# The first norm of a two-layer trunk: its squares, its sums and the loading of its rows

## Chip, core and metric

The kernel runs on one core of a Trainium2 chip. The metric is device time in microseconds (us). The engines are TensorE (PE: matmuls, with weight loads shown apart as PEld), VectorE (DVE), ScalarE (ACT), GpSimd (POOL) and SyncE (SP, which here only issues DMAs). L272 is line 272 of the kernel before.

## What is computed

A trunk of two layers over 512 tokens with 1024 features. Each layer is a mixer (layer 0: HGRN2 beside RWKV7; layer 1: attention), an MLP and a gate. What the change touches is the first step of layer 0, the RMS norm of the input and the projections behind it:

```python
def rms_norm(x, g, eps=NORM_EPS):
    xf = x.astype(jnp.float32)
    y = xf * lax.rsqrt(jnp.mean(xf * xf, axis=-1, keepdims=True) + eps)
    return (y * g.astype(jnp.float32)).astype(x.dtype)
...
    h = rms_norm(x, attn_norm[l])
    ...
    u = (h @ w_in).astype(jnp.float32)   # the input of both mixers
```

## The kernel before

The activations are kept with the features on the partitions: `x[k]`, k = 0 to 7, is a tile of 128 features by 512 tokens (256 KB), here called a row of the input. Matmuls of full precision are made of three passes: each operand is split into a high half, rounded on ACT (`act` L272, weights `whi` L228), and a low half, the remainder, made on DVE (L273, `wlo` L229); `mm3` (L235) then multiplies high by high (L236), high by low (L237) and low by high (L238). One output tile of a projection takes 8 x 3 matmuls of 512 columns. They are summed over the 8 rows in a PSUM bank (`pj` has 2 banks, `pmh` 2, `pmr` 4).

The norm isn't applied before the projections. The rows are split with only the gain as a scale. The projections run on them, and the reciprocal root of the mean square, one number for each token, is multiplied in when a projection is evacuated (`mixed` L417, `proj_h` L851). For this it is needed as a broadcast tile `rb` (128 x 512).

The sum of squares is formed in two steps. `NormAcc.add` (L301) squares a row, on ACT (L304) for odd k and on DVE (L306) for even k. The first square is the accumulator, and POOL adds the seven others to it (L310). The squares after the first come from the ring `E`, which has 4 buffers. At the end `NormAcc.rs` makes one `Stats` with one `add` (L281): four matmuls, with 128 tokens of the accumulator as weights and a column of ones as the moving operand, so that PSUM has the sums with the tokens on the partitions. Each of these four leaves two records in the trace. A dozen small DVE operations (L292 and `rsqrt`, L253) make the reciprocal root, four transposes on PE (L325) broadcast it, and ACT copies it to `rb` (L334). Other norms of the kernel use the same classes; `NormAcc` stays in use there.

Loading: one tile of weights is two pieces of 256 KB (`wnext`, L214), each issued on SP's queue and then split. There are two buffers for raw pieces (`wr`) and three for split ones. SP issues in this order: the vectors, x0, the first weight piece, x1 and x2, the second piece, x3 to x7, then the weights that follow. POOL's queue loads the constants and masks, and POOL first clears several tiles (L375, L378).

The order of the instructions on each engine is made ahead of the run by a scheduler, which takes what is ready by its own account of time, first in the program first, and gives out the buffers of the pools. At run time each engine keeps to this order and waits where something is not ready. The program's order around the change is: loads, split and square of each row, the end of the norm, masks (L399 on), the two LoRA projections (L840, `first` is the weight tile that was loaded early), then `proj_rkv(0)` (L876), `pre_h(0)` and `p1(0, 0)` of the first RWKV head (L898), and the rest of layer 0 in `step` (L899). `pre` (L456) starts with a matmul (L463) on the evacuated first LoRA projection `lwa`; in it the key norm `kk` goes through a `Stats` of its own (L474), `rsqrt` and transposes.

Of the kernel before, what the change touches and what calls it, by code (L numbers as in the profile page):

```python
# [17 lines left out]
AF = mybir.ActivationFunctionType  # L18
# [159 lines left out]
def trunk(ctx, tc, wts, xT, pT, vecs, lora, cst, lev, seg, rope, out, upto="all", dbg=None, mode=None):  # L178
# [97 lines left out]
    class Stats:  # L276
        def __init__(self, pool, tag, cols=1):
            self.n, self.cols, self.i = 1, cols, 0
            self.ps = pool.tile([P, 512], F32, name=tag)
# [48 lines left out]
    def norm_finish(st, tag):  # L328
        return norm_rows(st.rs(tag))

    def norm_rows(rt):
        ps = bcast_rows(rt, 1, pmh, "pmh")
        rb = nrm.tile([P, S], F32, name="rb")
        A.copy(rb, ps)  # L334
        return rt, rb
# [17 lines left out]

    # ------------------------------------------------------------------ layer 0: mixers
    def layer0_mixer(actp):
# [15 lines left out]
        SB = mp.tile([P, 9, P], F32, name="SB")  # L371
        PP = mp.tile([P, 4, P], F16, name="PP")
        early = [BH, KAs, *NAs, *BZ, GB, SB, PP]
        for t in early[:NE]:
# [4 lines left out]

        # norm of the input  # L380
        nc.sync.dma_start(vec, vecs)
        rest = iter(range(8))

        def load(n):
            for _ in range(n):
                k = next(rest)
                nc.sync.dma_start(x[k], xT[:, k, :])
        load(X0)
        first = wnext("in", WI["l", 0], lambda: load(X1))
        load(8 - X0 - 2 * X1)  # L390
        xs = []
        st = NormAcc(E)
        for k in range(8):
            xs.append(split(actp, x[k], "act", vcol("an0", k)))
            st.add(x[k], "act" if k % 2 else "dve")
        rt, rb = norm_finish(st, "n")

        # masks
        m32 = mp.tile([P, 14 * P // 4], I32, name="m32")  # L399
# [56 lines left out]
        def pre(hp, r, k, v):  # L456
            lw = E("lw", 2, [P, 3, P])
            ld = nc.gpsimd.dma_start(lw, lora[:, :, hp * P:hp * P + P])
            if hp == 0:
                tc.keep_in_program_order(ld)  # L460
            # decay
            ps = pmr.tile([P, S], F32, name="pmr")
# [4 lines left out]
            yield  # L467
            # kk
            kk = E()
# [7 lines left out]
            yield  # L477
            # a
            ps = pmr.tile([P, S], F32, name="pmr")
# [39 lines left out]
        def p1(hp, g):  # L519
            lw, bh, kh, ar, rh_, bo, dl, v, y = pre_[hp]  # L520
            gs = slice(g * 256, g * 256 + 256)
            NA, KA, TOK = NAs[g], KAs, []
            un[hp, g] = (NA, TOK)
            # score blocks, transposed
            for n, (src, dst) in enumerate(((bh, NA), (kh, KA))):
                for h in range(2):
                    A.copy(BH[hs[h], n, :, hs[h]], src[hs[h], gs].rearrange("p (c t) -> p c t", t=64))
                ps = pmr.tile([P, S], F32, name="pmr")
                for c_ in range(4):
                    o = g * 256 + c_ * 64  # L530
                    T.matmul(ps[:, c_ * P:c_ * P + P].rearrange("p (x t) -> p x t", x=2), BH[:, n, c_, :],  # L531
                             ar[:, :, o:o + 64], start=True, stop=True)
                pv = ps.rearrange("p (a c x t) -> p a c x t", a=2, c=2, x=2)
                for h in range(2):
                    for c_ in range(2):
                        V.tensor_tensor(dst[hs[c_], :, h, :, hs[c_]], pv[hs[h], :, c_, :, :],
                                        tri[hs[h], None, :, :].to_broadcast([64, 2, 2, 64]), op=OP.mult)
                yield
            for a in range(2):
                j = 2 * g + a  # L540
                js = slice(j * P, j * P + P)
                # token-major forms
                ps = pmr.tile([P, S], F32, name="pmr")
                for n, src in enumerate((ar[:, 0, :], v, bh, kh)):
                    T.transpose(ps[:, n * P:n * P + P], src[:, js], ident)
                t = E("TOK", 4, [P, 3, P])
                pv = ps.rearrange("p (x f) -> p x f", x=4)
                A.copy(t[:, 0:2, :], pv[:, 0:2, :])
                for c_ in range(2):
                    A.copy(BZ[g][hs[c_], a, :, c_, :], pv[hs[c_], 2:4, :])  # L550
                TOK.append(t)
                yield
            # A_ak V and A_rk V
            ps = pmr.tile([P, S], F32, name="pmr")
            for i, (a, h) in enumerate(pk):
                T.matmul(ps[:, i * 64:i * 64 + 64], KA[:, a, h, 0, :], TOK[a][:, 1, hs[h]], start=True, stop=True)
            for a in range(2):
                A.copy(TOK[a][:, 2, :], ps[:, a * P:a * P + P])
            yield
            ps = pmr.tile([P, S], F32, name="pmr")  # L560
            for i, (a, h) in enumerate(pk):
                T.matmul(ps[hs[h], a * P:a * P + P], TOK[a][:, 1, hs[h]], KA[:, a, h, 1, :], start=True, stop=True)
            A.copy(y[:, gs], ps[:, :256])
            yield

        def p2(hp, g):
            NA, TOK = un[hp, g]
            # inverse of I - N, per chunk
            n16 = E("n16", 1, [P, 4, P], F16)
# [47 lines left out]
            yield  # L617
            # T [alpha, A_ak V]
            ps = pmr.tile([P, S], F32, name="pmr")
# [9 lines left out]
        def p3(hp, g):  # L629
            lw, bh, kh, ar, rh_, bo, dl, v, y = pre_[hp]  # L630
            NA, TOK, MU = un.pop((hp, g))
            gs = slice(g * 256, g * 256 + 256)
            # the chunks' maps of the state
            HS = E("HS", 1, [P, 4, 64])
# [17 lines left out]

            # receptance with the state's share; outputs inside the chunks
            def inner():
# [35 lines left out]
        def tail(hp):  # L690
            lw, bh, kh, ar, rh_, bo, dl, v, y = pre_.pop(hp)
            dump(f"y{hp}", y)
            # head norm, bonus, gate
            ps = pmr.tile([P, S], F32, name="pmr")
# [28 lines left out]

        # ---------------- HGRN2
        KS = [mp.tile([P, S], F32, name=f"KS{i}") for i in range(2)]
# [4 lines left out]
        def hgrn(h, q, ff, iv, gproj):  # L730
            """q, g: half of the columns' values; ff: tanh(hf / 2); iv: the inputs."""
            vt = E("vt", 1, [P, NJ, P])
# [13 lines left out]
            V.tensor_tensor_scan(b, s128, ff, 0.0, op0=OP.mult, op1=OP.add)  # L746
            # within blocks of 128 tokens: blocks of four, then pairs of blocks
            at = E("at", 1, [P, NJ, P])
# [16 lines left out]
            for l in range(2, 7):  # L765
# [19 lines left out]
                def hi(t):  # L785
                    return t.rearrange("p i (n u) -> p i n u", u=2 * H)[:, :, :, H:]
                V.copy_predicated(hi(at), hi(m8[:, l:l + 1, :]).to_broadcast([P, NJ, 64 // H, H]),
                                  ps[:, :256].rearrange("p (i n u) -> p i n u", i=NJ, u=H))
            # across blocks
            d = Hh()  # L790
# [42 lines left out]

        # ---------------- order of work
        acc, xg = NormAcc(E), []
# [40 lines left out]
        proj_rkv(0)  # L876
        # lower bound of the forget gate: softmax over the rows, first row
        lbo = VEC["lb"][0]
# [51 lines left out]

    # ------------------------------------------------------------------ the rest
    later = []
# [305 lines left out]
```

## Time and profile before

| | us |
|---|---|
| runs: median of 3 (lowest to highest) | 1536.19 (1535.04 to 1536.39) |
| profiled execution: span, first to last instruction | 1533.0 |
| PE busy in the span | 1481.4 (97%) |
| DVE busy | 959.1 (63%) |
| ACT busy | 674.0 (44%) |
| POOL busy | 179.5 (12%) |

The run's time has what lies around the span besides the span itself; the median of the runs is 3.2 us above the profiled span. Matmuls are pipelined, so a busy PE may still be limited by its clock; what one matmul costs is read from the distance between starts. A view by stages gives the busy time of each engine in a stretch, and a view in order of time gives the start, the duration, and, in brackets, the idle time before an instruction with what ended it.

### The profile page before, as it was taken

The numbers are of one execution on the slowest core, as the hardware profiler recorded it, in microseconds if no ns is written. First come the engines' busy times: TensorE is split into PE (matmuls) and PEld (weight loads), VectorE is DVE, ScalarE is ACT, GpSimd is POOL, SyncE is SP. The second block draws the span as 40 slices with busy tenths as digits, with TensorE's granted clock in tenths as the row PEclk, the third lists the DMA queues.
The fourth block names the chain that finished last, engine by engine and source line by source line (L and its number), as shares of the span: only waits on it lengthen the run. The fifth ranks groups of instructions, "written<-read, shape, count | busy, mean of one in ns | idle before, by whom it ended". The sixth has DMA issues, their size and how long they took to land.

```text
span 1533.0 us, 20544 instructions
## 1 busy us (share of the span) xinstructions
PE 1481.4 (97%) x7532; PEld 1192.6 (78%) x7532; DVE 959.1 (63%) x1808; ACT 674.0 (44%) x1286; POOL 179.5 (12%) x161
## 2 busy tenths in 40 slices
PE   7999999999989999999999998999999999999998
PEld 5687787777768888888888886666778888888887
DVE  5877687687776644444456728888575444444463
ACT  3574555554446333333334445555634333333342
POOL 5221231211223000000000101111320000000000
PEclk9999999999999999999999999999999999999999
DMA  4210111211124333333333431111223333333331
GB/s 151 81 42 29 41 42 40 70 28 49 35 76 124 92 99 97 97 97 96 97 97 96 140 96 56 55 49 49 82 79 95 97 97 100 97 99 96 97 97 69
DMA packets 66965, 123.62 MB, mean 81 GB/s; under 512 B 7616, under 2 KB 8000, under 8 KB 66864
## 3 DMA queue, kind: packets, MB, share of 16 engines
q1 hardware_dynamic: 65376, 118.57, 25.6%
q10 hardware_dynamic: 1008, 2.16, 0.5%
q0 software_dynamic: 480, 1.57, 0.3%
q8 instruction: 59, 0.97, 0.3%
q14 instruction: 42, 0.34, 0.1%
HBM read 120.18 MB, written 2.10 MB: 80 GB/s over the span
## 4 chain that ended last, share of the span: by engine, by line
PE 84%; DVE 9%; ACT 3%; issue 2%; POOL 1%; DMA 1%; SPq 0%; DVEq 0%; ACTq 0%; POOLq 0%
PE pj L236 21%; PE pj L237 20%; PE pj L238 20%; PE pmr L237 2%; PE pmr L238 1%; PE pmr L236 1%; DVE wlo L229 1%; PE pmr L1135 1%; PE pmr L595 1%; PE pmh L783 1%; PE pmr L1159 1%; PE pmr L531 1%; DVE act L273 1%; PE pmr L638 1%; PE pmh L283 1%
## 5 line engine op out<-in xcount | busy, mean ns | idle before, releaser
L228 ACT CAST whi<-wr 128x512 fp32r<-128x512 f32 x436 | 270.2, 621 | 592.5 <-PE pj L237 479.8
L229 DVE TENSOR_TENSOR wlo<-wr,whi 128x512 fp32r<-128x512 f32 x436 | 318.1, 732 | 196.1 <-ACT whi L228 187.3
L236 PE MATMUL pj<-act,whi 128*128 128x512 f32 (+1 forms) x968 | 382.8, 396 | 0.9 <-DVE h L857 0.9
L237 PE MATMUL pj<-act,whi 128*128 128x512 f32 (+1 forms) x968 | 380.6, 393 | 0.0
L238 PE MATMUL pj<-act,wlo 128*128 128x512 f32 (+1 forms) x968 | 380.1, 393 | 0.5 <-DVE wlo L229 0.5
L236 PEld LDWEIGHTS pj<-act,whi 128*128 128x128 f32 x968 | 182.6, 189 | 38.5 <-issue 2.3
L238 PEld LDWEIGHTS pj<-act,wlo 128*128 128x128 f32 x968 | 182.4, 188 | 37.2 <-issue 1.2
L237 PEld LDWEIGHTS pj<-act,whi 128*128 128x128 f32 x968 | 182.6, 189 | 35.8 <-issue 1.2
L236 PE MATMUL pj<-hid,whi 128*128 128x512 f32 x512 | 199.2, 389 | 0.0
L237 PE MATMUL pj<-hid,whi 128*128 128x512 f32 x512 | 199.2, 389 | 0.0
L238 PE MATMUL pj<-hid,wlo 128*128 128x512 f32 x512 | 199.2, 389 | 0.0
L1032 DVE TENSOR_TENSOR x<-x,pj 128x512 f32<-128x512 f32 x128 | 88.1, 688 | 80.5 <-PE pj L238 80.1
L236 PEld LDWEIGHTS pj<-hid,whi 128*128 128x128 f32 x512 | 96.1, 188 | 20.2
L237 PEld LDWEIGHTS pj<-hid,whi 128*128 128x128 f32 x512 | 96.1, 188 | 19.9
L238 PEld LDWEIGHTS pj<-hid,wlo 128*128 128x128 f32 x512 | 96.1, 188 | 19.8
L1021 DVE SCALAR_TENSOR_TENSOR r<-pj,rb 128x512 f32<-128x512 f32 x56 | 38.7, 692 | 86.6 <-PE pj L238 86.6
L310 POOL TENSOR_TENSOR acc<-acc,xsq 128x512 f32<-128x512 f32 x28 | 38.6, 1380 | 435.7 <-ACT xsq L304 410.0
L270 DVE TENSOR_TENSOR hid<-r,hid 128x512 fp32r<-128x512 f32 x64 | 44.3, 693 | 43.2 <-ACT hid L269 43.2
L236 PE MATMUL pmr<-act,whi 128*128 128x512 f32 x112 | 46.1, 416 | 5.8 <-ACT whi L228 5.8
L237 PE MATMUL pmr<-act,whi 128*128 128x512 f32 x112 | 46.0, 414 | 4.6 <-DVE act L273 4.6
L1022 ACT ACTIVATE r<-r 128x512 f32<-128x512 f32 x64 | 40.4, 632 | 21.0 <-DVE r L1021 21.0
L238 PE MATMUL pmr<-act,wlo 128*128 128x512 f32 x112 | 45.1, 407 | 0.0
(402 smaller groups left out, 2059.3 us busy)
## 6 DMA issues: line engine op xcount, KB each, us to landing
wr<-in_wts_dram SPq DMA_DIRECT2D x436, 256.0 KB, 2.7
x<-in_xT_dram SPq DMA_DIRECT2D x8, 256.0 KB, 5.9
out_dram<-x SPq DMA_DIRECT2D x7, 256.0 KB, 2.0
r<-in_pT_dram ACTq DMA_DIRECT2D x4, 256.0 KB, 3.6
lw<-in_lora_dram POOLq DMA_DIRECT2D x4, 192.0 KB, 3.2
tqn<-in_rope_dram ACTq DMA_DIRECT2D x1, 512.0 KB, 4.9
tkn<-in_rope_dram ACTq DMA_DIRECT2D x1, 512.0 KB, 5.5
cs<-in_cst_dram POOLq DMA_DIRECT2D x1, 289.0 KB, 7.3
```

The lines of the kernel that those rows point to most:

```text
L228: A.copy(hi, raw)
L229: V.tensor_sub(lo, raw, hi.bitcast(F32))
L236: T.matmul(ps, wh, xh, start=first, stop=False)
L237: T.matmul(ps, wh, xl, start=False, stop=False)
L238: T.matmul(ps, wl, xh, start=False, stop=last)
L270: V.tensor_sub(l, src, h.bitcast(F32))
L273: V.scalar_tensor_tensor(l, src, scale, h.bitcast(F32), op0=OP.mult, op1=OP.subtract)
L283: T.matmul(self.ps[:, j * self.cols:(j + 1) * self.cols], sq[:, j * P:(j + 1) * P], rhs, start=(self.i == 0 and j == 0), stop=(self.i == s ...
L310: G.tensor_add(self.t, self.t, sq)
L1021: V.scalar_tensor_tensor(r, q, 0.0, nf[0], op0=OP.max, op1=OP.mult)
L1022: A.activation(r, r, AF.Square)
L1032: V.tensor_add(x[k], x[k], ps)
```

## The change

Rows x0, x1, x3 and x5 are issued on ACT's queue; x2, x4, x6 and x7 stay on SP's, x2 behind the first weight piece and x4 behind the second. The squares of all eight rows are made on ACT, into the ring `E`. Each square goes at once into four one-column matmuls, which sum over the partitions and, over the eight rows, in one PSUM bank of `pmh`. So the first norm has no DVE squares, no POOL adds and no accumulator in SBUF; it has 32 of these matmuls instead of 4. `Stats` takes the number of additions as `n`. The hunks that are left out only take comments away.

```diff
     class Stats:
-        def __init__(self, pool, tag, cols=1):
-            self.n, self.cols, self.i = 1, cols, 0
+        def __init__(self, pool, tag, cols=1, n=1):
+            self.n, self.cols, self.i = n, cols, 0
             self.ps = pool.tile([P, 512], F32, name=tag)
...
         PP = mp.tile([P, 4, P], F16, name="PP")
+        XS = [(2,), (4,)]
...
-        rest = iter(range(8))
-
-        def load(n):
-            for _ in range(n):
-                k = next(rest)
-                nc.sync.dma_start(x[k], xT[:, k, :])
-        load(X0)
-        first = wnext("in", WI["l", 0], lambda: load(X1))
-        load(8 - X0 - 2 * X1)
+        load(nc.scalar, 0)
+        first = wnext("in", WI["l", 0], lambda: load(nc.sync, *XS.pop(0)))
+        load(nc.scalar, 1, 3, 5)
+        load(nc.sync, 6, 7)
         xs = []
-        st = NormAcc(E)
+        st = Stats(pmh, "pmh", n=8)
         for k in range(8):
             xs.append(split(actp, x[k], "act", vcol("an0", k)))
-            st.add(x[k], "act" if k % 2 else "dve")
-        rt, rb = norm_finish(st, "n")
+            sq = E()
+            A.activation(sq, x[k], AF.Square)
+            st.add(sq, ones)
+        rt, rb = norm_rows(st.rs(1.0 / D, EPS, "n"))
```

The new `load(eng, *ks)` issues `x[k]` on the given engine's queue for each k.

## Rows read from the trace of the kernel before

**Rows 1.** Busy time by stages: us, then each engine's busy us, PEclk, DMA, GB/s.

```profile
0.00:20.00 20.00, 10.55 (x23) 6.38 (x24) 16.54 (x32) 10.51 (x17) 15.88 (x23) 0.85 0.60 199
...
60.00:100.00 40.00, 36.97 (x272) 29.50 (x272) 33.32 (x72) 26.27 (x63) 12.38 (x13) 1.00 0.16 43
```

**Rows 2.** TensorE in order of time: start us, us, engine, line, operation.

```profile
5.83 0.79 PE L236 MATMUL pmr<-act,whi 128*128 128x512 f32 x1 [5.83 <-ACT whi L228]
...
10.18 0.66 PE L236 MATMUL pmr<-act,whi 128*128 128x512 f32 x1
12.73 0.50 PE L237 MATMUL pmr<-act,whi 128*128 128x512 f32 x1 [1.89 <-DVE act L273]
...
15.20 0.80 PE L237 MATMUL pmr<-act,whi 128*128 128x512 f32 x1 [1.50 <-DVE act L273]
...
17.07 0.79 PE L237 MATMUL pmr<-act,whi 128*128 128x512 f32 x1 [0.23 <-DVE act L273]
...
20.65 0.46 PE L238 MATMUL pmr<-act,wlo 128*128 128x512 f32 x1
```

**Rows 3.** Busy time by finer stages, columns as in rows 1.

```profile
5.00:10.60 5.60, 4.77 (x10) 2.71 (x10) 4.93 (x10) 4.44 (x10) 5.56 (x8) 1.00 0.98 338
...
17.00:20.70 3.70, 3.63 (x9) 2.85 (x10) 2.97 (x9) 0.00 (x0) 0.00 (x0) 0.50 0.11 33
```

**Rows 4.** Chain that ended last, in order of time: start us, us, what.

```profile
19.57 0.85 PE pmr L236 x2
...
31.14 0.45 PE pmr L238 x2
...
35.81 0.79 PE pmh L283 x8
```

**Rows 5.** VectorE and GpSimd in order of time: around an add, and last row.

```profile
10.78 1.89 DVE L273 SCALAR_TENSOR_TENSOR act<-x,vec,act 128x512 fp32r<-128x512 f32 x1
10.84 1.28 POOL L310 TENSOR_TENSOR acc<-acc,e 128x512 f32<-128x512 f32 x1
...
17.88 0.74 DVE L273 SCALAR_TENSOR_TENSOR act<-x,vec,act 128x512 fp32r<-128x512 f32 x1
```

**Rows 6.** In order of time: last adds on GpSimd, first evacuation on VectorE.

```profile
25.54 2.66 POOL L310 TENSOR_TENSOR acc<-acc,e 128x512 f32<-128x512 f32 x2
...
43.75 0.69 DVE L419 TENSOR_TENSOR u<-pmr,rb 128x512 f32<-128x512 f32 x1
```

**Rows 7.** What TensorE waited for, 40 to 60 us: total us, times, longest.

```profile
PE pj L236 <- DVE h L857: 0.9, 1, 0.9
PE pmr L463 <- ACT k L421: 0.7, 1, 0.7
```

**Rows 8.** ScalarE in order of time: first row; high half, square, high half.

```profile
4.39 0.72 ACT L272 ACTIVATE act<-x,vec 128x512 fp32r<-128x512 f32 x1 [2.16 <-DMA x<-in_xT_dram]
...
6.22 0.72 ACT L272 ACTIVATE act<-x,vec 128x512 fp32r<-128x512 f32 x1 [0.44 <-DMA x<-in_xT_dram]
...
6.85 0.61 ACT L304 ACTIVATE e<-x 128x512 f32<-128x512 f32 x1
...
7.37 0.71 ACT L272 ACTIVATE act<-x,vec 128x512 fp32r<-128x512 f32 x1
```

**Rows 9.** DMA issues: first row on SP; one line's issues on ScalarE (ns).

```profile
1.19 0.42 SPq L387 DMA_DIRECT2D x<-in_xT_dram  x1
...
L953 ACTq DMA_DIRECT2D r<-in_pT_dram x4: 334/356/451, 463.8 to 873.6; - x4
```

**Rows 10.** TensorE's weight loads in order of time: half clock, then full clock.

```profile
17.24 0.34 PEld L238 LDWEIGHTS pmr<-act,wlo 128*128 128x128 f32 x1
...
21.18 0.19 PEld L236 LDWEIGHTS pmr<-act,whi 128*128 128x128 f32 x1
```

**Rows 11.** First head's key norm: start on VectorE; transposes (chain that ended last).

```profile
59.06 0.17 DVE L294 TENSOR_SCALAR m_kk<-pmr 128x8 f32<-128x8 f32 x1 [0.38 <-PE pmr L283]
...
66.66 0.67 PE pmr L325 x4
```

More of the change, by code (lines that the diff above doesn't have):

```diff
@@ L378, in layer0_mixer, with load @@
             G.memset(t, 0.0)
+        def load(eng, *ks):
+            for k in ks:
+                eng.dma_start(x[k], xT[:, k, :])
         nc.sync.dma_start(vec, vecs)
-        rest = iter(range(8))
-        def load(n):
-            for _ in range(n):
-                k = next(rest)
-                nc.sync.dma_start(x[k], xT[:, k, :])
-        load(X0)
-        first = wnext("in", WI["l", 0], lambda: load(X1))
-        load(8 - X0 - 2 * X1)
+        load(nc.scalar, 0)
+        first = wnext("in", WI["l", 0], lambda: load(nc.sync, *XS.pop(0)))
+        load(nc.scalar, 1, 3, 5)
+        load(nc.sync, 6, 7)
         xs = []
-        st = NormAcc(E)
+        st = Stats(pmh, "pmh", n=8)
         for k in range(8):
             xs.append(split(actp, x[k], "act", vcol("an0", k)))
-            st.add(x[k], "act" if k % 2 else "dve")
-        rt, rb = norm_finish(st, "n")
+            sq = E()
+            A.activation(sq, x[k], AF.Square)
+            st.add(sq, ones)
+        rt, rb = norm_rows(st.rs(1.0 / D, EPS, "n"))
         m32 = mp.tile([P, 14 * P // 4], I32, name="m32")
```

## The prediction

> **What bounds the kernel now.** I read the busy time by stages first, to find where TensorE (PE) is not kept busy, since elsewhere nothing that this change touches can be gained. PE has 10.55 busy us in the first 20, and 36.97 in the 40 from 60 to 100 [rows 1]; from 17 to 50 it hardly pauses, and neither does it in the long layers after 460. So the first norm sits in the one place where PE idles much, and the reader should ask why it idles there.
>
> PE's own order of time answers that. Its first matmul starts at 5.83, when the first weight piece has been rounded. Then come ten matmuls, a hole that ends at 12.73, another that ends at 15.20, and a last small one before 17.07; from there it runs on [rows 2]. The holes at 12.73 and 15.20 wait for the low halves of the input rows (L273), made by VectorE (DVE). PE also runs at the lower of its two clocks (1.2 instead of 2.4 GHz; half clock below) for part of this: the matmul at 10.18 still takes 0.66, the one at 12.73 takes 0.50, those at 15.20 and 20.65 are slow again, and the granted clock of 17.0 to 20.7 is 0.50 [rows 2, 3]. At half clock a full matmul costs 0.425 us start to start, at full clock 0.225 [rows 4].
>
> DVE is late because of the adds on GpSimd (POOL): a low half that takes 0.74 alone takes 1.89 while an add of 1.28 runs [rows 5]. Three more DVE operations of this stretch are drawn out in the same way (a weight's low half, a square, a cast). DVE makes the last low half at 17.88 [rows 5].
>
> A second thing to see is that the norm ends late. POOL is through at 25.54 + 2.66 = 28.20, but the first evacuation that needs the broadcast norm starts at 43.75 [rows 6]. By then several projections wait in PSUM, DVE has to catch up, and PE waits 0.9 and 0.7 us for it [rows 7].
>
> **The change, part by part.** *Removed:* seven POOL adds and four DVE squares. POOL is no bound, so the adds are worth nothing by themselves; the gain is that DVE loses three squares before 17 us and the stretching of four operations (1.89 - 0.74 = 1.15 us for the one shown). The cover for row splitting then goes to the next engine.
>
> *Added on ScalarE (ACT):* four squares more and four DMA issues. High half to square is 6.85 - 6.22 = 0.63 start to start, square to the next 7.37 - 6.85 = 0.52 [rows 8], so one row costs ACT 1.15. Eight rows are 9.2, two weight roundings in between at most 0.6 each, taken like a high half, so ACT ends near 4.4 + 9.2 + 1.2 = 14.8, if the first row starts where it does now. The last low half follows by 0.74, at about 15, against 17.88 + 0.74 = 18.6. DVE needs 8 x 0.74 plus two weight halves of about the same in these 10 us and keeps up.
>
> *The queues.* An issue on ACT's queue took 0.36 [rows 9]; four are 1.4 us in ACT's order. I put them at nothing, because ACT now waits for the first row until 4.39 [rows 8] with little to do; without that cover (the first row issued behind the table load and the warm-up) row 0 comes up to 1 us later. On SP the first weight piece is no longer behind x0, whose issue took 0.42 [rows 9], so PE may start at 5.83 - 0.42 = 5.41. The later rows move past each other, but 338 GB/s went through with DMA engines 0.98 busy from 5 to 10.6 [rows 3], so I give the second queue no bandwidth. The Trainium skill says the same more strongly ("DMA: Bandwidth & Descriptors", section "Issuing engines are not separate DMA queues"): transfers begun on several engines run on the same 16 DMA engines, and what is saved is issue time; by it the "two queues" part is worth those 0.42 us, and if it were wrong the rows would come sooner, which ACT at 1.15 a row could not use.
>
> *Added on PE:* one group of four one-column sums becomes eight groups. The present group is eight records in 0.79 us at full clock [rows 4], so seven more are 5.5 us. The trace has no such group at half clock. A lower bound is 0.79; doubling gives 1.58; weight loads take 0.34 against 0.19 [rows 10], and, assuming that a one-column matmul is mostly its weight load, I take 0.79 x 0.34 / 0.19 = 1.4. A row of the first LoRA projection with its sums then costs PE 3 x 0.425 + 1.4 = 2.7 at half and 3 x 0.225 + 0.79 = 1.48 at full clock. Both are above ACT's 1.15, so after the first row PE no longer starves: PE is late next. It now waits on squares, and the projection's matmuls stand behind such a wait; the four square buffers make ACT's square k wait for PE's group k - 4, which at these rates is met just in time.
>
> *Front sum.* I take full clock from 10.6, because now the matmul at 10.18 is slow after starting at 5.83, and the next one after the hole is faster. From 5.41 to 10.6 are 5.2 / 2.7 = 1.9 rows; the other 6.1 rows and one matmul take 6.1 x 1.48 + 0.23 = 9.2, so 25 matmuls and all sums end at 19.8. Today the 25th matmul starts at 20.65 [rows 2] and takes some 0.3 until the next, and the group of 0.79 is still to come: 21.7 for equal work. Gain 1.9. Ends: half clock until 13 gives 20.9 (gain 0.8), full clock from the start 17.5 (gain 4.2).
>
> *Evacuations.* From the sums (35.81 + 0.79 = 36.6) to the first evacuation at 43.75 the trace has 7.2 us, small DVE operations, a transpose and a copy, with other work between; from 19.8 on, this puts the norm near 24 to 27, so the projections are evacuated as they finish. I count the two waits of 0.9 and 0.7 [rows 7] as gone: 1.6. Bounds 0 (PE waits elsewhere) and 1.6.
>
> *Sum.* 1.9 + 1.6 = 3.5 us. Profiled span 1533.0; the three runs have a median 3.2 above it, which I take as constant: span 1529.5, **time 1532.7**. Bounds by the ends above: gain 0.8 to 5.8, 1530.4 to 1535.4.
>
> **Rivals.** (1) *The first RWKV head starts earlier too.* PE has 40 - 36.97 = 3.0 idle us between 60 and 100 [rows 1], in the chain that begins after the norm. With the norm some 17 us earlier, this chain has more projections to hide behind: 3.5 + 3.0 = 6.5, 1529.7. Against it: the order on each engine is fixed ahead of the run, and holes may only move.
>
> (2) *The sums don't fill the holes.* If the fixed order puts them behind the projection, the low halves alone still finish PE's first projection near 15.7 (24 x 0.425 from 5.41), but then 8 x 0.79 come on top: 15.7 + 0.2 + 6.3 = 22.2 against 21.7, a loss of 0.5; with the 1.6, a gain of 1.1, 1535.1. The same result if the front gain comes but PE's waits at 50 us reappear elsewhere (1.9, 1534.3). This is also what is left if the change does less than it says.
>
> (3) *Slower: the clock stays at half.* The sum groups leave the array little to stream. If PE stays at half through all eight rows, it ends at 5.41 + 8 x 2.7 + 0.4 = 27.4, a loss of 5.7; less 1.6 is 4.1, 1540.3. For it: PE is at half clock for much of this stretch today. Against it: today it falls after holes, and here are none; from 60 us on, 272 mostly small matmuls in 40 us run at 1.00 [rows 1]. It becomes slower than 0.2% only if half clock lasts to about 25 us; half until 20.65, as today, costs 2.7 in front and ends within 0.2%.
>
> (4) *Slower: the head's chain is pulled into PE's order.* The key norm of the first head goes from 59.06 on DVE to the transposes at 66.66 on PE [rows 11], 7.6 us that projections cover today. If the new order has the transposes earlier with few projections between, PE waits for that chain: 3.5 - 7.6 = 4.1 slower, 1540.3. It decides from about 6.6 us of new waiting.
>
> **How the numbers follow.** Forecast 0.45, rival (1) 0.17, rival (2) 0.21, (3) 0.08, (4) 0.09. A measurement of this kernel tells about 0.2%, 3.07 us, from no change. The forecast lies just beyond that: of its 0.45 I put 0.28 above and 0.17 within. Faster 0.28 + 0.17 = 0.45; same 0.17 + 0.21 = 0.38; slower 0.17. The range goes from a little beyond rival (1) to rivals (3) and (4): 1528.5 to 1540.3; the forecast's own is 1530.4 to 1535.4.
>
> **What the profile would show.** Right: no DVE operation near 1.9 in the first 17 us; last low half near 15; PE without holes from 5.4; groups of sums of 0.8 to 1.6 between its matmuls; granted clock 1.00 from about 10.6 on; first evacuation at 24 to 27; no wait at 50 to 54. Wrong: first row split after 5.4 (issues on ACT behind the table load); granted clock 0.50 beyond 20; sums behind the projection; or PE's idle time between 60 and 460 us changed by more than 3 us, since the order there is remade as a whole.

## The result, and the profile after

The changed kernel takes 1553.48 us (median of 4 runs, 1551.51 to 1555.62); the kernel before, on the same chip, 1535.99. The ratio is 1.0115, with an interval of 1.010 to 1.0129: slower by 17.5 us, where 1532.7 was forecast and 1540.3 was the upper end of the range. The profiled spans are 1549.7 and 1533.0, so 16.7 us are to be found in the trace.

Where they arise is read from the busy time by stages, cut at three places that both traces have: the first evacuation that reads the broadcast norm from a "pj" bank (49.96 before, 63.42 after), the first update of x by the mixer (228.0, 244.7), and the last one (459.6, 476.3). The first two of these stages, of the kernel before, then of after; columns as in [rows 1]:

```profile
0.00:50.00 50.00, 40.47 (x156) 30.29 (x156) 31.00 (x62) 21.13 (x35) 20.78 (x28) 0.93 0.44 140
50.00:228.00 178.00, 169.05 (x1230) 136.45 (x1230) 141.49 (x331) 102.74 (x229) 45.44 (x48) 1.00 0.14 44
```

```profile
0.00:63.40 63.40, 54.24 (x212) 45.49 (x212) 24.72 (x59) 23.11 (x40) 12.96 (x23) 1.00 0.33 110
63.40:244.70 181.30, 172.17 (x1230) 136.89 (x1230) 140.46 (x330) 103.25 (x228) 44.32 (x45) 1.00 0.14 43
```

The first stage lost 13.4 us. The second lost 3.3: the same 1230 TensorE records, 172.17 - 169.05 = 3.1 us more busy, and equal idle time (9.13 against 8.95). Behind that nothing differs: the third stage is 231.6 in both, and the rest too is equal. In the first stage PE's idle time is about the same (9.2 against 9.5) and its busy time is 13.8 us longer, for 56 records more: the seven added groups of sums, which at full clock would be 5.5 us.

TensorE (PE) in order of time, after, which answers to [rows 2]:

```profile
9.06 0.80 PE L236 MATMUL pmr<-act,whi 128*128 128x512 f32 x1 [9.06 <-ACT act L272]
9.66 1.79 PE L283 MATMUL pmh<-ones,e 128*128 128x1 f32 x8
11.51 0.79 PE L237 MATMUL pmr<-act,whi 128*128 128x512 f32 x1
...
12.52 1.70 PE L283 MATMUL pmh<-ones,e 128*128 128x1 f32 x8
14.08 0.78 PE L236 MATMUL pmr<-act,whi 128*128 128x512 f32 x1
...
15.51 1.70 PE L283 MATMUL pmh<-ones,e 128*128 128x1 f32 x8
...
33.00 0.63 PE L238 MATMUL pmr<-act,wlo 128*128 128x512 f32 x1
33.43 0.63 PE L236 MATMUL pmr<-act,whi 128*128 128x512 f32 x1
...
37.23 0.40 PE L236 MATMUL pmr<-act,whi 128*128 128x512 f32 x1
37.46 0.39 PE L237 MATMUL pmr<-act,whi 128*128 128x512 f32 x1
```

Three things are to be seen. PE starts at 9.06, not at 5.83 or the forecast 5.41. From there it hardly pauses, yet its matmuls are 0.42 to 0.43 apart (33.00 to 33.43): half clock, until 37.23, where they come 0.23 apart. And a row, three matmuls and one group, costs 2.99 us (from the group at 12.52 to the one at 15.51), of which 1.56 lie between the start of a group and the next matmul (12.52 to 14.08). The 24 matmuls of the first projection and the sums end at 33.43, and with a 25th matmul at 33.86; the same 25 and the sums ended at 21.7 before.

ScalarE (ACT) and VectorE (DVE) show the late start:

```profile
5.48 0.62 ACT L228 CAST whi<-wr 128x512 fp32r<-128x512 f32 x1 [2.81 <-DMA wr<-in_wts_dram]
...
7.77 0.62 ACT L228 CAST whi<-wr 128x512 fp32r<-128x512 f32 x1 [1.67 <-DMA wr<-in_wts_dram]
8.29 0.72 ACT L272 ACTIVATE act<-x,vec 128x512 fp32r<-128x512 f32 x1
...
17.30 0.63 ACT L395 ACTIVATE e<-x 128x512 f32<-128x512 f32 x1 [1.50 <-PE pmh L283]
```

```profile
9.85 1.58 DVE L415 CAST id<-cs 128x128 f16<-128x128 f32 x1 [0.74 <-DMA cs<-in_cst_dram]
9.99 1.44 DVE L273 SCALAR_TENSOR_TENSOR act<-x,vec,act 128x512 fp32r<-128x512 f32 x1
...
11.67 2.73 DVE L273 SCALAR_TENSOR_TENSOR act<-x,vec,act 128x512 fp32r<-128x512 f32 x4
...
39.17 0.69 DVE L420 TENSOR_TENSOR u<-pmr,rb 128x512 f32<-128x512 f32 x1 [1.56 <-ACT rb L334]
```

ACT's order, made anew, has both weight roundings ahead of row 0, and the second waits for its DMA until 7.77; row 0 is split at 8.29, against 4.39 before [rows 8]. On DVE the cast of the identity now stands ahead of the first low half and waits for the constants' DMA until 9.85. The low half is done at 11.43 and PE's second matmul starts at 11.51; this costs only 0.3 us, since the group that starts at 9.66 holds PE for 1.56 us anyway. Behind that the drawn-out low halves are gone (four in 2.73 us), and the first evacuation comes at 39.17 instead of 43.75 [rows 6].

One column of the profile misleads here: the same stretch of after, and then of the experiment preheat below, which runs the same matmuls there at the same 0.43 apart:

```profile
20.00:30.00 10.00, 10.00 (x37) 9.06 (x38) 0.00 (x0) 1.77 (x4) 0.00 (x0) 1.00 0.01 2
```

```profile
20.00:30.00 10.00, 10.00 (x36) 8.94 (x37) 0.00 (x0) 1.77 (x4) 0.00 (x0) 0.50 0.01 2
```

The granted clock reads 1.00 in the first and 0.50 in the second. The clock of preheat had gone up and down before, that of after had not yet changed; up to the first change the column seems to stand at 1.00 whatever the clock is. There the distance between matmuls is what tells it, and the prediction's sign for half clock, a granted clock of 0.50 beyond 20, doesn't show although half clock is there.

### The profile page after: what moved, and what is told of

Its sections match the earlier page's. It is cut to its first block, busy times and chain, and to the rows that moved or that the text cites. A ratio compares the mean times of both kernels' runs of the same rounds, so it can differ in the third digit from the quotient of the medians.

```text
span 1549.7 us, 20649 instructions
## 1 busy us (share of the span) xinstructions
PE 1498.2 (97%) x7588; PEld 1208.8 (78%) x7588; DVE 951.4 (61%) x1804; ACT 676.5 (44%) x1290; POOL 170.5 (11%) x154
## 4 chain that ended last, share of the span: by engine, by line
PE 85%; DVE 8%; ACT 3%; issue 2%; POOL 1%; DMA 1%; DVEq 0%; ACTq 0%; POOLq 0%
PE pj L236 21%; PE pj L238 20%; PE pj L237 20%; PE pmr L237 2%; PE pmr L236 2%; PE pmr L238 2%; PE pmh L283 1%; PE pmr L1136 1%; PE pmr L596 1%; PE pmr L532 1%; DVE wlo L229 1%; PE pmh L784 1%; PE pmr L1160 1%; DVE act L273 1%; PE pmr L639 1%
## 5 line engine op out<-in xcount | busy, mean ns | idle before, releaser
L238 PEld LDWEIGHTS pj<-act,wlo 128*128 128x128 f32 x968 | 182.6, 189 | 38.1 <-issue 1.7
L236 PE MATMUL pmr<-act,whi 128*128 128x512 f32 x112 | 47.6, 425 | 9.1 <-ACT act L272 9.1
L237 PE MATMUL pmr<-act,whi 128*128 128x512 f32 x112 | 47.6, 427 | 1.1 <-DVE act L273 1.0
```

Of the source, the lines that this page charges most:

```text
L236: T.matmul(ps, wh, xh, start=first, stop=False)
L237: T.matmul(ps, wh, xl, start=False, stop=False)
L238: T.matmul(ps, wl, xh, start=False, stop=last)
```

## The experiments

Theory A: the one-column sums keep TensorE at half clock. Rivals: the late start by the queues; work added on PE at any clock; an order that is worse by chance. All runs were timed against the kernel before, whose medians beside them were 1535.2 to 1536.6. The sums stand in different places in each free order, so the first three kernels write the order out: for each row three matmuls of the first projection, then its sum. They keep the loads of the kernel before.

**pin_narrow**: squares on ACT, one-column sums, order pinned.

```diff
+        def sums(k):
+            for j in range(NJ):
+                keep(T.matmul(st.ps[:, j:j + 1], sqs[k][:, j * P:j * P + P], ones, start=(k == 0 and j == 0),
+                              stop=k == 7, skip_group_check=True))
+
         for k in range(8):
             xs.append(split(actp, x[k], "act", vcol("an0", k)))
-            st.add(x[k], "act" if k % 2 else "dve")
-        rt, rb = norm_finish(st, "n")
+            sqs.append(E())
+            A.activation(sqs[k], x[k], AF.Square)
...
+            keep(T.matmul(ps0, hi, xh, start=k == 0, stop=False))
+            keep(T.matmul(ps0, hi, xl, start=False, stop=False))
+            keep(T.matmul(ps0, lo, xh, start=False, stop=k == 7))
+            sums(k)
+        rt, rb = norm_rows(st.rs(1.0 / D, EPS, "n"))
```

> Rows load as before, on SP alone; squares on ACT and one-column sums on PE as in the change; TensorE's order is pinned: three matmuls of a row of the first projection, then that row's four one-column sums, eight times. Theory A (the one-column sums between the matmuls keep TensorE at its low clock): start near 5.8 us, about 3.0 us a row to the end of the eighth row near 30, full clock only some 3 to 4 us after the last sum, 1543 to 1549 us. Rival B (the sums cost only their own time; the loss of the change comes from its loads and late start): about 1.5 us a row from 10 us on, eighth row done near 20 to 21, 1533 to 1538 us. Rival C (the loss is made later, by the remade order of layer 0): the front like B, and still over 1545.

1553.1 us, ratio 1.011 (1.0095 to 1.0125). PE in order of time:

```profile
7.10 0.79 PE L408 MATMUL pmr<-act,whi 128*128 128x512 f32 x1 [7.10 <-ACT whi L228]
...
8.54 1.70 PE L399 MATMUL pmh<-ones,e 128*128 128x1 f32 x8
10.10 0.78 PE L408 MATMUL pmr<-act,whi 128*128 128x512 f32 x1
...
33.29 0.63 PE L238 MATMUL pmr<-act,wlo 128*128 128x512 f32 x1
33.71 0.51 PE L236 MATMUL pmr<-act,whi 128*128 128x512 f32 x1
34.06 0.39 PE L237 MATMUL pmr<-act,whi 128*128 128x512 f32 x1
```

Half clock for all eight rows and until 34.06, 2.99 a row (8.54 to 10.10, then three matmuls), though it starts two us earlier and has no queue changed: the loss is with the sums. The time is 4 us above A's range.

**pin_wide**: the same order; each row's sum is four matmuls of 512 columns with a matrix of ones. It leaves the right sum out (each square is counted four times); PE gets more to stream, not less. Against pin_narrow:

```diff
         def sums(k):
-            for j in range(NJ):
-                keep(T.matmul(st.ps[:, j:j + 1], sqs[k][:, j * P:j * P + P], ones, start=(k == 0 and j == 0),
-                              stop=k == 7, skip_group_check=True))
+            for i in range(4):
+                keep(T.matmul(st.ps, onesw, sqs[k], start=(k == 0 and i == 0), stop=(k == 7 and i == 3)))
...
-            sqs.append(E())
+            sqs.append(E(dt=F32R))
```

`onesw` is a matrix of 128 x 128 ones in fp32r.

> As pin_narrow, with the same pinned order, but each row's sum is made by four 512-column matmuls with a 128x128 matrix of ones instead of four one-column matmuls (single pass; the values are not the norm: the sum is counted four times, and what is read off for the norm is the wrong part of it). These four take about as long on TensorE as the one-column group (4 x 0.225 = 0.9 us at full clock, 4 x 0.425 = 1.7 at half). Theory A (the low clock comes from how little the one-column group streams): the clock rises by about 10 to 12 us as in the kernel before, then 1.6 us a row, eighth row done near 20 to 22, 1533 to 1539 us, some 9 us less than pin_narrow. Rival B (nothing of the clock, time is the same work): equal to pin_narrow within 2 us.

1542.0 us, ratio 1.0039 (1.0024 to 1.0053).

```profile
7.17 0.80 PE L411 MATMUL pmr<-act,whi 128*128 128x512 f32 x1 [7.17 <-ACT whi L228]
...
8.62 1.91 PE L403 MATMUL pmh<-e,onesw 128*128 128x512 f32 x4
...
10.75 0.46 PE L412 MATMUL pmr<-act,whi 128*128 128x512 f32 x1
11.05 0.39 PE L413 MATMUL pmr<-act,wlo 128*128 128x512 f32 x1
11.28 1.07 PE L403 MATMUL pmh<-e,onesw 128*128 128x512 f32 x4
```

The same start and the same order, and full clock from 10.75 on; a row goes from 2.99 to 1.63, and the time falls by 11 us. So the form of the sum holds the clock down, not sums on PE as such. In both traces PE is busy without a pause up to there; what differs is the four instructions behind each third matmul. They differ in several things at once (one column or 512, the squares or the ones as weights, fp32 with two records each or fp32r), which no run separates. The clock is as A has it; the time is 3 us above A's range, because behind the first stage (51.2 us) 6 us more go than before (181.3 and 234.3). The Trainium skill ("TensorE: Matmul & The Clock Gate", Part 1) says that the array is throttled by default and that activity releases it. The runs agree, and show beside it that a stretch of 26 us in which the profile counts PE as busy can pass without that release.

**pin_late**: as pin_narrow, but all eight groups behind the 24 matmuls. Against pin_narrow:

```diff
-            sqs.append(E())
+            sqs.append(E() if k < 4 else Hh())
...
-            sums(k)
+        for k in range(8):
+            sums(k)
```

> As pin_narrow, but all eight groups of one-column sums stand behind the first projection's 24 matmuls (four more buffers for the squares). Theory A: the 24 matmuls raise the clock as in the kernel before and are done near 17 us; the 64 records of the sums then take 6.3 us if the clock is up when they start (end near 23, 1535 to 1539), 12 us if it is not or falls (end near 29, 1541 to 1546). Rival B: 1533 to 1538.

1551.6 us, ratio 1.0097 (1.0078 to 1.0117).

```profile
16.48 0.43 PE L409 MATMUL pmr<-act,whi 128*128 128x512 f32 x1
16.74 0.40 PE L410 MATMUL pmr<-act,wlo 128*128 128x512 f32 x1
...
18.34 3.63 PE L399 MATMUL pmh<-ones,e 128*128 128x1 f32 x32
21.83 5.58 PE L399 MATMUL pmh<-ones,h 128*128 128x1 f32 x32
27.27 0.77 PE L236 MATMUL pmr<-act,whi 128*128 128x512 f32 x1
```

Without sums between them the matmuls reach full clock at 16.48, and the last starts at 18.11, in spite of a hole of 2.2 us (DVE's cast waiting for the constants). Then comes a run of one-column matmuls alone: its first half takes 3.49 (18.34 to 21.83), its second 5.44 at a granted clock of 0.64, and the matmul behind it is at half clock. No wait stands in this run. A run of one-column matmuls alone thus loses a clock that was up. A allowed for this, but the time is 6 us above its range (1541 to 1546); the profiled execution, 1547.3, is the fastest of the four.

**load_only**: the two queues alone; squares, adds and sums as before.

> Only the second part of the change: rows over two queues, with the norm's squares on ACT and DVE and its adds on POOL as before. ACT's order has both weight roundings ahead of the first row's split here too. Theory A with a late start: TensorE's first matmul near 9 us instead of 5.8, no sums in between, loss of 2 to 4 us: 1537 to 1541. If the loads and the late start were the main cause (rival B): 1546 or more. If the start costs nothing because the row splitting is what bounds: 1534 to 1537.

1541.0 us, ratio 1.0033 (1.002 to 1.0047).

```profile
8.43 0.80 PE L236 MATMUL pmr<-act,whi 128*128 128x512 f32 x1 [8.43 <-ACT act L272]
```

The queues bring no gain: they cost 4.7 us (1536.3 beside them), through the same order on ACT as in after (both roundings ahead of row 0), and 3.1 us of that is in the first stage (53.1). The Trainium skill's rule on issuing engines that the prediction cited ("DMA: Bandwidth & Descriptors", section "Issuing engines are not separate DMA queues") agrees: the DMA engines are 1.01 busy from 5 to 10.6 us, as they were before (0.98, [rows 3]), and the second queue made nothing faster. The loss lies in the order of the issuing engine.

**sums_only**: the other half alone, order free, loads as before.

> The second half of the change alone: squares on ScalarE and one-column sums in PSUM, with the loads of the kernel before, all on one queue, and the order left free. It tells what the queues add to the sums. Under the theory that the clock is all: first matmul 6 to 7 us instead of 9.06, half clock to 33 or later, 1550 to 1554 us, so that the two queues, worth 4.4 us by themselves (1541.0), add 0 to 3 here. Rival (the late start by the queues is what keeps the clock down): clock up by 15, 1540 to 1545 us.

1551.7 us, ratio 1.0109 (1.0092 to 1.0126). PE starts at 6.40, with a group of sums, and is at half clock until 33.02. The halves cost 4.7 and 16.5 us alone and 17.5 together: the sums are nearly all of it, and the two don't add up.

**row0_first**: the changed kernel, row 0 split ahead of the first weight in the program.

```diff
+        xs = [split(actp, x[0], "act", vcol("an0", 0))]
         first = wnext("in", WI["l", 0], lambda: load(nc.sync, *XS.pop(0)))
...
-            xs.append(split(actp, x[k], "act", vcol("an0", k)))
+            if k:
+                xs.append(split(actp, x[k], "act", vcol("an0", k)))
```

> The changed kernel with row 0 split ahead of the first weight, in program order, so that ScalarE's order has row 0's high half ahead of the first weight's rounding, which waits for its DMA. This is for the late start alone (first matmul at 9.06 instead of 5.83). Expected first matmul 6 to 7 us. If the late start is a term of its own beside the clock: 2 to 3 us less than the changed kernel, 1550 to 1552. If the clock alone counts and the start is absorbed (ScalarE's squares, then the rows, are late anyway): within 1 us of the changed kernel, 1553 to 1554. In both the rows stay near 3.0 us each at half clock.

1553.0 us, ratio 1.0114 (1.0099 to 1.0129). PE starts at 6.19, 2.9 us earlier than after, waits 0.95 for the first square, and reaches full clock at 35.77 instead of 37.23. The first "pj" evacuation comes 1.7 us earlier (61.71), but the second stage then takes 182.6 and the third 233.1, 1.3 and 1.5 more than in after. By the sum the second expectation is right, by the way it comes about neither: the early start was worth 1.7 and was lost again behind the front, in stretches that the edit doesn't touch. The third stage's part is an extra fall of the clock, which stands in late_adds at the same place (0.66 in the five us from 200 us into the stage, in both); all eleven experiments take 232.8 to 234.3 there, whatever their edit, and the traced executions of before and after 231.6.

**preheat**: the changed kernel with 26 matmuls on a tile of ones ahead of everything, to have the clock up at 9 us.

```diff
...
+        for i in range(26):
+            T.matmul(hp_, heat[:, :P], heat, start=True, stop=True)
```

> The changed kernel with 26 extra matmuls of 512 bf16 columns on TensorE at the start, whose result nobody reads: they fill TensorE from about 1.5 to 9 us, so the clock is up when the first real matmul starts at about 9. Everything else is as in the changed kernel. Theory A (a stretch made up largely of one-column sums lets the clock fall even when it is up): the first rows run at 1.5 to 1.6 us each, then matmuls are 0.425 apart again before the eighth row is through; 1546 to 1552 us. Rival B (the clock only has to be brought up once, and the sums then hold it because TensorE is always busy): matmuls stay 0.225 apart, the 24th starts near 21, 1539 to 1543 us.

1550.8 us, ratio 1.0086 (1.0061 to 1.011), and the seven runs fall into two sorts: five from 1549.9 to 1553.3 with a mean granted clock of 0.988 to 0.990, and two at 1541.1 and 1542.2 with 0.997. The profiled run is of the first sort; behind a hole of 0.91 at 12.55 the matmuls were 0.43 apart. The time is in A's range, but neither A nor its rival explains both sorts, so the next two kernels were to take the hole away.

**preheat_pin** and **preheat_long**: pin_narrow with 20 and with 40 such matmuls. With 40 the real work starts 5 us late, so that all rows are ready by their turn.

> The kernel with the pinned order of three matmuls and four one-column sums a row (1553.1), with 20 extra matmuls of 512 bf16 columns ahead of the first real one at about 7, so that the clock is up when the rows begin and no hole lies between. In the first kernel with such extra matmuls the profiled execution lost the clock at about 12, behind a hole of 0.91 us, yet two of its seven runs took 1541 to 1542. A (the stretch of one-column sums lets the clock fall by itself): half clock again within the eight rows, rows of 3.0, 1547 to 1553 us. B (only a hole lets it fall; sums without holes hold it): rows of 1.5 all through, the 24th matmul near 20, 1538 to 1542 us.

> The same with 40 extra matmuls: TensorE is kept streaming to about 12, by when most rows are split and squared, so the eight rows can run without a hole at either clock. It starts the real work some 5 us late. A: the clock falls within the eight rows in spite of that: rows of 1.5 turn into 3.0, 1552 to 1558 us. B: rows of 1.5 to the end, the last sum at 12 + 8 x 1.5 = 24, 1541 to 1545 us.

preheat_pin: 1551.1 us, ratio 1.0087 (1.0053 to 1.0122); three runs from 1550.9 to 1552.8, one at 1540.2 with a mean granted clock of 0.997. preheat_long: 1543.3, all four from 1542.7 to 1544.3, ratio 1.0052 (1.0037 to 1.0067). PE in the one, then in the other:

```profile
10.42 0.95 PE L404 MATMUL pmh<-ones,e 128*128 128x1 f32 x8
11.23 0.48 PE L413 MATMUL pmr<-act,whi 128*128 128x512 f32 x1
12.57 0.50 PE L414 MATMUL pmr<-act,whi 128*128 128x512 f32 x1 [0.87 <-DVE act L273]
...
13.22 1.70 PE L404 MATMUL pmh<-ones,e 128*128 128x1 f32 x8
14.78 0.77 PE L413 MATMUL pmr<-act,whi 128*128 128x512 f32 x1
```

```profile
12.17 0.58 PE L413 MATMUL pmr<-act,whi 128*128 128x512 f32 x1
...
13.06 0.95 PE L404 MATMUL pmh<-ones,e 128*128 128x1 f32 x8
13.87 0.49 PE L413 MATMUL pmr<-act,whi 128*128 128x512 f32 x1
...
24.26 0.95 PE L404 MATMUL pmh<-ones,e 128*128 128x1 f32 x8
25.07 0.49 PE L236 MATMUL pmr<-act,whi 128*128 128x512 f32 x1
```

Without a hole the clock stays up through all eight rows, 1.60 us each: for the mix of three matmuls and one group, theory A in the form "the sums let the clock fall" is wrong, and rival B right. In preheat_pin a hole of 0.87 us came after all, and the clock falls behind it (the group at 13.22 takes 1.56 to the next matmul, that at 10.42 took 0.81), and stays down to the end of the rows. A hole alone needn't do that: one of 1.18 us in load_only (up to 30.82) and one of 1.56 in late_adds below (up to 16.34), among matmuls of 512 columns, leave these 0.23 to 0.24 apart, though in the kernel before two close together, 1.89 and 1.50, were followed by a fall [rows 2]. So the state decides: this mix holds a clock that is up, can't raise one that is down (pin_narrow, after), and has little to spare for a hole. preheat_long also streams 20 matmuls more beforehand, which isn't separated from the missing hole. In the one short run of preheat_pin, and the two of preheat, the clock presumably outlasted the hole; only their times and mean clocks say so, as there is no trace of them.

**late_adds**, made to beat both kernels: loads, adds on POOL and one last group of sums as before, but all squares on ACT behind the eight row splits, so that no add runs beside a low half; DVE's cast of the identity goes behind the last low half.

```diff
+        for k in range(8):
+            xs.append(split(actp, x[k], "act", vcol("an0", k)))
+        keep(V.tensor_copy(id16, ident))
         st = NormAcc(E)
         for k in range(8):
-            xs.append(split(actp, x[k], "act", vcol("an0", k)))
-            st.add(x[k], "act" if k % 2 else "dve")
+            sq = nrm.tile([P, S], F32, name="acc") if k == 0 else E()
+            keep(A.activation(sq, x[k], AF.Square))
+            if k:
+                G.tensor_add(st.t, st.t, sq)
...
```

> Meant to be faster than both kernels: the loads of the kernel before and its POOL adds and one last group of sums stay, but all eight squares are made on ScalarE behind the eight row splits, so that no add of POOL runs while VectorE makes the low halves; the cast of the identity, which waits for a DMA, is put behind the last low half. Theory (VectorE drawn out by POOL's adds makes the holes; TensorE then goes to full clock like the kernel with wide sums): low halves 0.74 each, no hole from 6 to 17, clock up near 11, the 24th matmul at 17 to 18 against some 20.4 before, 1530 to 1534 us. Rival (the order of layer 0 is remade, and the other kernels lost 2 to 5 us there between 50 and 480 whatever the front did): 1535 to 1540 us in spite of the front gain.

1534.8 us (10 runs), ratio 0.9987 (0.9978 to 0.9996): faster than the kernel before by 1.8 us, the fastest here, by little. It lies between the theory's range and the rival's.

```profile
11.86 2.11 DVE L273 SCALAR_TENSOR_TENSOR act<-x,vec,act 128x512 fp32r<-128x512 f32 x3 [0.67 <-ACT act L272]
...
16.32 2.85 DVE L229 TENSOR_TENSOR wlo<-wr,whi 128x512 fp32r<-128x512 f32 x2 [1.89 <-ACT whi L228]
```

```profile
14.39 0.39 PE L238 MATMUL pmr<-act,wlo 128*128 128x512 f32 x1
16.34 0.50 PE L236 MATMUL pmr<-act,whi 128*128 128x512 f32 x1 [1.56 <-ACT whi L228]
16.68 0.40 PE L237 MATMUL pmr<-act,whi 128*128 128x512 f32 x1
```

The low halves are 0.70 apart and done at 13.97, against 18.62 before; the clock is up near 10, and PE's 24th matmul starts at 14.39, its 25th at 16.34, where the 25th started at 20.65 before [rows 2]. This fits the prediction's reading of the holes by [rows 5], though DVE's squares and the cast have left this stretch with the adds, so the share of each isn't separated; that adds draw DVE out is seen again at 16.32, where two low halves of weights take 2.85 beside them (1.28 alone, at 18.54 before). The Trainium skill ("SBUF — State Buffer", section "Who interferes with whom") has the rule behind it: a VectorE instruction with two inputs in SBUF contends with a GpSimd instruction that reads there; the low half has two such inputs, and takes 1.89 beside an add and 0.70 without. But of those 4.3 us only 2.4 arrive at the first evacuation (41.38 against 43.75), since PE now waits for the next weights: up to 16.34 for a rounding that stands behind five squares in ACT's order (13.09 to 15.78), 0.47 us for the drawn-out low half behind it, and 0.60 up to 26.39 for a later one, whose chain goes through a DMA that ACT awaits for 3.43 us up to 20.24. Behind the second stage another 1.5 go, for that extra fall of the clock (0.66 from 425 to 430; no such fall stands in the trace of the kernel before until 453).

**wide_one**: one matmul of 512 columns a row for the sum, in the pinned order; the norm is then two ACT operations.

> The sums in a form that streams: for each row, one matmul of 512 columns with a matrix of ones against the square, rounded to fp32r, in the pinned order (three matmuls of the row, then its sum); it leaves the sum on all partitions, so the norm is two ScalarE operations and no transposes. Loads as before. Theory A (what kept the clock down is the one-column form, not that sums are made on TensorE): clock up near 11, four matmuls a row, the last sum at about 7 + 9 x 0.425 + 23 x 0.225 = 16 to 18, first evacuation before 25; 1531 to 1537 us, the upper half if the remade order of layer 0 costs 2 to 5 us as in the kernel with four wide matmuls a row (1542.0), below 1536 if it does not. If sums on TensorE in any form keep the clock down: 1545 or more.

1539.4 us (10 runs), ratio 1.0016 (1.0006 to 1.0025). The clock is up at 10.4, the last sum is done at 17.8, and the first evacuation comes at 21.83, as A has it. But the norm's two table loads (1.28 each) stand in ACT's order ahead of a weight's rounding, PE has a hole of 2.19 up to 23.84, and the clock is down for 3.5 us behind it; the second stage takes 182.3 and the third 234.1. So the time is above the 1531 to 1537 that A had. The form that streams takes 14 us less than the change, and is still 2.8 us slower than the kernel before.

## Why the prediction was wrong

*What bounds the kernel now* stands: in late_adds, without adds beside the low halves, the holes are gone. That they are worth little is what the prediction missed there: the next thing late behind them is the next weights, with their rounding, low halves and DMA.

*Front sum* is the step that failed. It took full clock from 10.6 "because now the matmul at 10.18 is slow after starting at 5.83, and the next one after the hole is faster". Before, the clock rose behind a run of ten matmuls of 512 columns with nothing else between (the one at 10.18 still takes 0.66, that at 13.06 0.40); the change puts a group of one-column matmuls behind every third. Rival (3) had this, with a chance of 0.08, and was set aside with two reasons. Of these, "today it falls after holes, and here are none" speaks of a clock that is up, and here it never came up. The 272 mostly small matmuls at 1.00 [rows 1] show that such work can keep a clock up, which preheat_long bears out, not that it can raise one.

The price of rival (3), a loss of 4.1, was too small as well. Its terms against the trace: the start, 9.06 for 5.41, 3.65; the row, 2.99 for 2.7, over eight rows 2.3; half clock not to the last sum but on to 37.23, nine matmuls at 0.2 extra, 1.8; the evacuations' gain of 1.6, which did not come; the second stage, 3.3. Together 4.1 + 12.7 = 16.8, and the spans differ by 16.7. So close a fit is partly luck: the 0.3 us at the first low half is in no term.

*Added on PE*: the group's 1.4 at half clock was an estimate between 0.79 and 1.58, and is 1.56; at full clock 0.81 for 0.79. The doubling was the better guess: at half the clock a one-column group takes nearly twice the time. The row at full clock, put at 1.48 (its own sum, 3 x 0.225 + 0.79, gives 1.465), is 1.60 in preheat_long, since the first matmul behind a group takes 0.32.

*The queues*: "at nothing" failed by its own condition. Row 0 was split at 8.29, far beyond the 5.4 named as the sign; not the issues did that (0.40 each) but the weight roundings ahead of row 0 in ACT's order. Alone the queues cost 4.7 us (load_only); with the sums there, an order that has row 0 first gains 1.7 us in the first stage (row0_first).

*Removed* and *Added on ACT* were right in size (1.13 a row, low halves 0.7 apart), but of no effect. ACT's last two squares wait for PE's sums, 1.50 and 2.17 us, as the four buffers make them; PE never waits for that. One reading fails: the cast of the identity takes 1.58 in after too, beside clears on POOL only, so it doesn't take an add to draw it out; with POOL idle it takes 0.22 (late_adds, 13.88).

*Evacuations*: the norm came 4.6 us earlier than before (first evacuation at 39.17 for 43.75), not at 24 to 27, since its sums ended late; the wait on L421 is gone, and the wait of 0.9 on L857 has become one of 0.5 on another evacuation. PE's idle time in the second stage stayed the same, 9.13 for 8.95, with waits for the LoRA weights' DMA of 3.4 in it (0.5 before). The gain was a wait exchanged for another.

*The second stage*, named in the last part as a thing to watch, cost 3.3 us in another way than idle time. PE's groups for the stretch by line, before and then after (records, busy us, mean ns):

```profile
L237 PE MATMUL pj<-act,whi 128*128 128x512 f32 x104 | 42.5, 409 | 0.0
L595 PE MATMUL pmr<-X,n 128*128 128x64 f16 x80 | 5.7, 194 | 0.5 <-DVE X L600 0.5
```

```profile
L237 PE MATMUL pj<-act,whi 128*128 128x512 f32 x104 | 43.5, 418 | 0.0
L596 PE MATMUL pmr<-X,n 128*128 128x64 f16 x80 | 6.9, 195 | 0.8 <-DVE X L601 0.7
```

The same operations, of the same mean where they are small, fill more time. All kernels with the row sums on PE have 181.3 to 182.6 us in this stretch, whatever their front did; load_only has 179.7, late_adds 178.2 and the same 169.1 busy as before. So it goes with the orders that come with the sums on PE. That large and small matmuls alternate more often, and overlap less, would explain it; that was not tried, and stays open.

Would the forecast have held with the clock up? preheat_long suggests not. Its eight rows take 12.9 us at full clock, so from 5.41 they and a 25th matmul would end near 18.5, a front gain of 3.2 against 21.7; the second stage takes 3.3 to 3.9 of it back. About 1536 is then likelier, near rival (2)'s 1535.1. This is worked out, not run.

## What to carry to other kernels

Before moving small sums onto TensorE, ask in which state the clock is at that place: at the start of a kernel they delayed the rise, between long matmuls they rode along with a clock that was up (preheat_long), a run of them alone lost it (pin_late), and a hole among them can cost the clock for the whole stretch. Give a reduction the form that streams (a matrix of ones as the stationary operand, the data as 512 moving columns), or keep it off TensorE until the clock is up; here even the form that streams came out behind the kernel before (wide_one), so the orders made anew count too. And where a DMA issue or a row goes to another engine, read that engine's whole order again: what waits there for something else now stands ahead of the row.

## What the runs showed of the hardware

TensorE stayed at half clock with no pause that the profile shows from 11.51 to 37.23 in after: three long matmuls and one group of one-column records a row did not raise it; with four long ones in place of the group (pin_wide) it rose at 10.75. The same mix held full clock from 12.17 to 25.07 once it was up. A run of one-column matmuls alone lost it between 18.34 and 27.27. A one-column group of eight records takes 0.81 us at full and 1.56 at half clock.
